# All weight operands of the first MLP's first unit made on ACT and POOL during the pooling, with sums in place

## The chip, the cores and the metric

The kernel runs on one core of a Trainium2 chip. Its five engines work from queues of their own, in order: PE (matrix products), DVE (vector), ACT (activations and copies), POOL (elementwise work on tiles in SBUF) and SP, which here issues every DMA. They wait for each other through semaphores. The metric is the device time of one execution in microseconds (us).

## The reference

Two residual layers on x of 1024 positions by 1024 channels, float32. Layer 0 mixes tokens by a centred pooling of four window sizes, layer 1 by differential attention. Each is followed by a gated MLP, and a root-mean-square norm stands ahead of each sub-layer:

```python
h = h + mixer(rms_norm(h, mix_norm[i]))
g, u = split(rms_norm(h, ffn_norm[i]) @ w_up[i], 2)      # 1024 -> 2 * 2816
gc = conv_b + sum(conv_w[j] * shifted(g, j))             # three taps along the sequence
h = h + (gelu(gc) * u) @ w_down[i]
```

After the second layer comes one more norm. Only layer 0, between its pooling and the first columns of its MLP, is touched by the change.

## The kernel before

**Precision.** A float32 operand of a product is split into two float32r tiles: hi is a copy made on ACT, lo is the operand less hi, made on DVE or POOL. A product is then three matmuls (hi·hi, lo·hi, hi·lo).

**The up projection.** The 2816 columns are worked in 22 units of 128 columns of g and 128 of u. A unit is a two by two block product, the channels in two halves and the sequence in two halves, done with seven products instead of eight (numbers 1 to 7; 12 matmuls of 128x512 each). The weight side needs seven operands: u1, u2, g2 as loaded, and four sums, s1 = g1+g2 (product 5), s2 = s1-u1 (product 6), u1-g1 (product 7), u2-s2 (product 3). Each is split into hi and lo. The x side needs seven as well: x1 and x2 come from the first four row tiles of 128 positions, x3 to x7 from sums of tiles 0 to 3 with tiles 4 to 7. PE runs the products of a unit in the order 1, 6, 2, 7, 5, 4, 3.

**Preparing a unit's weights.** `load` issues the two loads of a unit's weights (`raw`, 512 KB each) on SP. `prep` is a generator that makes the seven operands. For unit 0 its four sums are on DVE (L394) and five of its seven lo parts too (L380); for later units sums and lo parts are on POOL. The sums go into buffers `s`, the parts into buffers `wc`.

**Around it.** The pooling goes by halves of the sequence. `pool_band` makes the pooled values as band products (L828), one block `pl` of 128 channels after the other, each split into hi (ACT, L131) and lo (DVE, L132). `pool_proj` multiplies one row tile of 128 positions (L848, accumulators `pp`), `add_halves` adds to the residual (DVE, L175) and squares (ACT, L176), `rstd` makes the norm's factor in small DVE and ACT steps (L188 to L198, `ss`, `ms`, `rt`, `rs_p`, `rs_q`, `rs_r`), and `norm_to_x` scales the rows (ACT, L292, `xs`), turns them on PE (L299, `tp`) and makes the x operands: products with the gain (`b`, L309 on DVE, L331 on ACT), for tiles 4 to 7 the sums `t`, `b`, `xf` (DVE, L340 to L344), then hi (ACT, L304) and lo (L305, on POOL for x1 to x4 and x7, on DVE for x5 and x6; x1 of the first layer on POOL too).

**Order.** In this stretch no order is written by hand: a scheduler lays the instructions into each engine's queue by priority and by its own idea of durations, and the queue then runs as it is laid. `next(mlp)` runs the MLP's generator up to its next `yield`, so that its instructions are recorded at that place in the program, ahead of `pool_band(1)`. From unit 1 on the order of PE, DVE and ACT is the written one. Buffers that are used again later make their next user wait: `cm`, `wd` and `g` belong to the up stage (sums of the gated values, the down weights, the g values of a unit); the raw weights of unit 0 of this layer lie in two of the three `g` buffers.

The accumulators of the attention, the rest of the up stage and the down stage are as they were, and so is each engine's order there.

## Time and profile before

| what | value |
|---|---|
| median of 3 runs | 2084.54 us (2083.7 to 2086.34) |
| the profiled execution's own time | 2089.84 us |
| its span, first to last instruction | 2088.0 us |
| mean granted clock | 0.983 |
| PE busy | 2003.6 us (96%) |
| DVE busy | 1560.6 us (75%) |
| ACT busy | 1024.4 us (49%) |
| POOL busy | 895.3 us (43%) |

A row of the timeline gives the start and the length in us, the engine, the line of the kernel, the operation, the tile written and the tiles read, and the shape; behind it in brackets stands how long the engine was idle before, and what ended that. An `xN` row is N such instructions in a row. Instructions on one engine follow each other a little faster than their lengths say, since the tail of one overlaps the head of the next. A row of the table of windows gives a stretch, its length, and for each engine the busy time and the number of instructions, then PE's granted clock, the DMA share and the GB/s.

### The profile page before, as it was taken

The numbers are of one execution on the slowest core, as the hardware profiler recorded it, in microseconds if no ns is written. First come the engines' busy times: TensorE is split into PE (matmuls) and PEld (weight loads), VectorE is DVE, ScalarE is ACT, GpSimd is POOL, SyncE is SP. The second block draws the span as 40 slices with busy tenths as digits, with TensorE's granted clock in tenths as the row PEclk, the third lists the DMA queues.
The fourth block names the chain that finished last, engine by engine and source line by source line (L and its number), as shares of the span: only waits on it lengthen the run. The fifth ranks groups of instructions, "written<-read, shape, count | busy, mean of one in ns | idle before, by whom it ended". The sixth has DMA issues, their size and how long they took to land.

```text
span 2088.0 us, 27647 instructions
## 1 busy us (share of the span) xinstructions
PE 2003.6 (96%) x9659; PEld 1665.6 (80%) x9659; DVE 1560.6 (75%) x2294; ACT 1024.4 (49%) x1838; POOL 895.3 (43%) x676
## 2 busy tenths in 40 slices
PE   5789999999999999999999998997999999999998
PEld 5768888888888877888888887875888888888886
DVE  6877777777665748899899888778667777775665
ACT  5743333333443645676667666456433333334443
POOL 4489999997000000101110110114999999930000
PEclk7889999999999999999999999999999999999999
DMA  4226445454876512122212115253345545458663
GB/s 153 99 70 198 141 154 184 132 177 151 334 239 221 207 56 66 48 75 61 61 46 77 54 35 197 101 172 118 121 160 167 172 149 179 142 191 334 201 211 132
DMA packets 221720, 301.90 MB, mean 145 GB/s; under 512 B 17852, under 2 KB 142092, under 8 KB 218764
## 3 DMA queue, kind: packets, MB, share of 16 engines
q1 hardware_dynamic: 221580, 300.13, 44.0%
q8 instruction: 76, 1.25, 0.2%
q14 instruction: 64, 0.52, 0.1%
HBM read 196.78 MB, written 90.70 MB: 138 GB/s over the span
## 4 chain that ended last, share of the span: by engine, by line
PE 59%; DVE 5%; ACT 2%; DMA 2%; issue 1%; SPq 1%; POOL 0%; ACTq 0%; DVEq 0%; POOLq 0%
PE dn L596 14%; PE up_b L422 8%; PE pj L1027 7%; PE up_c L422 5%; PE up_a L422 5%; PE sc L1113 5%; PE pj L1069 4%; PE po L1155 3%; PE aT L1144 3%; PE pj L1251 2%; DVE nm L1115 1%; DMA kf<-t 1%; ACT prob L1118 1%; DMA raw<-in_ffn_w_up_dram 0%; PE wo_acc L1251 0%
## 5 line engine op out<-in xcount | busy, mean ns | idle before, releaser
L1095 POOL TENSOR_TENSOR q_lo<-qt,q_hi 128x256 fp32r<-128x256 f32 x64 | 49.6, 776 | 683.4 <-ACT q_hi L1094 351.0
L380 POOL TENSOR_TENSOR w_lo<-s,w_hi 128x512 fp32r<-128x512 f32 x168 | 273.9, 1630 | 17.7 <-ACT w_hi L379 17.2
L596 PE MATMUL dn<-hnT_hi 128*128 128x512 f32 x560 | 218.3, 390 | 0.4 <-DVE hda L617 0.2
L596 PE MATMUL dn<-hnT_lo,hnT_hi 128*128 128x512 f32 x560 | 217.9, 389 | 0.0
L596 PE MATMUL dn<-hnT_hi,hnT_lo 128*128 128x512 f32 x560 | 217.9, 389 | 0.0
L422 PE MATMUL up_b<-x_hi,w_hi 128*128 128x512 f32 x528 | 207.2, 392 | 5.8 <-ACT x_hi L304 4.6
L422 PE MATMUL up_b<-x_lo,w_hi 128*128 128x512 f32 x528 | 206.4, 391 | 2.3 <-DVE x_lo L305 2.3
L380 POOL TENSOR_TENSOR w_lo<-raw,w_hi 128x512 fp32r<-128x512 f32 x130 | 195.1, 1501 | 30.0 <-ACT w_hi L379 26.5
L422 PE MATMUL up_b<-x_hi,w_lo 128*128 128x512 f32 x528 | 206.2, 391 | 0.0
L379 ACT CAST w_hi<-s 128x512 fp32r<-128x512 f32 x176 | 108.4, 616 | 179.1 <-PE up_b L422 87.3
L1115 DVE TENSOR_REDUCE nm<-sc 128x1 f32<-128x1024 f32 x128 | 155.8, 1217 | 15.7 <-PE sc L1113 15.0
L579 ACT CAST hnT_hi<-mst 128x1024 fp32r<-128x1024 f32 (+1 forms) x76 | 74.7, 983 | 164.7 <-PE dn L596 123.1
L1118 ACT ACTIVATE prob<-sc,nm 128x1024 f32<-128x1024 f32 x128 | 142.7, 1115 | 23.3 <-DVE nm L1115 11.6
L580 DVE TENSOR_TENSOR hnT_lo<-mst,hnT_hi 128x1024 fp32r<-128x1024 f32 (+1 forms) x76 | 86.5, 1138 | 90.1 <-ACT hnT_hi L579 90.1
L422 PE MATMUL up_a<-hnT_hi,w_hi 128*128 128x512 f32 x352 | 139.3, 396 | 1.4 <-ACT g L499 0.9
L422 PE MATMUL up_a<-hnT_lo,w_hi 128*128 128x512 f32 x352 | 138.8, 394 | 0.1
L422 PE MATMUL up_a<-hnT_hi,w_lo 128*128 128x512 f32 x352 | 138.5, 394 | 0.0
L394 POOL TENSOR_TENSOR s<-raw 128x512 f32<-128x512 f32 x84 | 133.1, 1584 | 10.3 <-DMA raw<-in_ffn_w_up_dram 4.1
L422 PE MATMUL up_c<-hnT_hi,w_lo 128*128 128x512 f32 x352 | 137.1, 389 | 0.3 <-DVE w_lo L380 0.3
L422 PE MATMUL up_c<-hnT_hi,w_hi 128*128 128x512 f32 x352 | 136.9, 389 | 0.0
L422 PE MATMUL up_c<-hnT_lo,w_hi 128*128 128x512 f32 x352 | 136.9, 389 | 0.0
L596 PEld LDWEIGHTS dn<-hnT_hi 128*128 128x128 f32 x560 | 105.1, 188 | 22.9 <-DVE hda L617 1.2
(304 smaller groups left out, 5433.3 us busy)
## 6 DMA issues: line engine op xcount, KB each, us to landing
raw<-in_ffn_w_up_dram SPq DMA_DIRECT2D x88, 512.0 KB, 4.3
mst<-m_dram SPq DMA_DIRECT2D x70, 512.0 KB, 6.2
wd<-in_ffn_w_down_dram SPq DMA_DIRECT2D x22, 1024.0 KB, 6.0
wd_dram<-wd SPq DMA_DIRECT2D x22, 1024.0 KB, 6.4
m_dram<-cm SPq DMA_DIRECT2D x80, 256.0 KB, 5.6
wst<-wd_dram SPq DMA_DIRECT2D x40, 512.0 KB, 4.8
m_dram<-gc SPq DMA_DIRECT2D x66, 256.0 KB, 6.3
wst<-in_ffn_w_down_dram SPq DMA_DIRECT2D x30, 512.0 KB, 7.2
```

The costliest lines, as they stand in the source:

```text
L379: A.copy(hi, src)
L380: eng.tensor_tensor(lo, src, f32(hi), ALU.subtract)
L394: eng.tensor_tensor(t, a, b, op)
L422: PE.matmul(acc, l[a][:, k], r[b][:, k], start=first and n == 0, stop=n == 11, skip_group_check=True)
L579: A.copy(h_, x)
L580: V.tensor_tensor(l_, x, f32(h_), ALU.subtract)
L596: PE.matmul(banks[t], l[:, q, cols], r[:, q], start=first and cnt == 0, stop=stop and cnt == 3 * n - 1, skip_group_check=True)
L1027: PE.matmul(acc, l[:, k % 2, h], r[:, k], start=(n == 0), stop=(n == 3 * NK - 1))
L1069: PE.matmul(acc, l[:, k % 4], r[:, k], start=(n == 0), stop=(n == 3 * NK - 1))
L1113: PE.matmul(sc[:, ns_], l[:, c], ks[:, c, ns_], start=(l is qhi), stop=(l is qlo))
L1115: V.tensor_reduce(nm, sc, AX.X, ALU.max, negate=True)
L1118: A.activation(soft[j, i][c], sc, AF.Exp, bias=nm, accum_out=sm[:, c, i:i + 1])
```

## The change

For layer 0 the new `prep_first` makes all seven operands of unit 0 instead of `prep(0)`. Every sum and every lo part is on POOL and every hi part on ACT, as before. The four sums are written in place over the raw weights, so that no `s` buffer is used. Only operands 1 and 2 take `wc` buffers; 7 and 5 go into the buffer `cm`, 4 and 3 into `wd`, 6 into the third `g` buffer. The first step (1, 2 and 4) is recorded with the raised priority that it had for 1 and 2, and a second `next(mlp)` records all the rest right behind it, still ahead of `pool_band(1)`. Before, the rest was recorded after the pooling. Layer 1 goes on using `prep(0)`.

```diff
+READY = (0,)
@@ ffn
+        def pairs(where):
+            if where in ("cm", "wd"):
+                t = ar.tile(where, [P, 2, 2, 4, P], F32R, "w_hl")
+                return [(t[:, i, 0], t[:, i, 1]) for i in range(2)]
+            if where == "g":
+                t = ar.tile(where, [P, 2, 4, P], F32R, "w_hl")
+                return [(t[:, 0], t[:, 1])]
+            return [tuple(ar.tile(where, [P, 4, P], F32R, n) for n in ("w_hi", "w_lo"))]
+
-        def parts(src, eng=G):
-            hi, lo = (ar.tile("wc", [P, 4, P], F32R, n) for n in ("w_hi", "w_lo"))
+        def parts(src, eng=G, into=None):
+            hi, lo = into or pairs("wc")[0]
             A.copy(hi, src)
             eng.tensor_tensor(lo, src, f32(hi), ALU.subtract)
             return hi, lo
+
+        def prep_first():
+            w = ws.setdefault(0, {})
+            ru, rg = raws.pop(0)
+            u1, u2, g1, g2 = ru[:, 0:4], ru[:, 4:8], rg[:, 0:4], rg[:, 4:8]
+            room = {}
+            (room[7], room[5]), (room[4], room[3]) = pairs("cm"), pairs("wd")
...
+                room[1], room[2] = pairs("wc") + pairs("wc")
+                room[6], = pairs("g")
+            w[1] = parts(u1, G, room[1])
+            if not layer:
+                w[2] = parts(u2, G, room[2])
+            w[4] = parts(g2, G, room[4])
+            yield
+            for o, x, y, op, i in ((g2, g1, g2, ALU.add, 5), (g1, u1, g1, ALU.subtract, 7),
+                                   (u1, g2, u1, ALU.subtract, 6)):
+                G.tensor_tensor(o, x, y, op)
+                if i == 6:
+                    w[6] = parts(o, G, room[6])
+            for i, o in ((7, g1), (5, g2)):
+                w[i] = parts(o, G, room[i])
...
+            G.tensor_tensor(u2, u2, u1, ALU.subtract)
+            w[3] = parts(u2, G, room[3])
@@ ffn, at its start
-        first = prep(0)
+        first = prep_first() if layer in READY else prep(0)
         next(first)
-        if layer:
+        if layer and layer not in READY:
             next(first)
         yield
+        if layer in READY:
+            next(first, None)
+            yield
         load(1)
@@ trunk_kernel, between the two halves of the pooling
     with tc.high_priority(offset=100):
         next(mlp)
+    next(mlp)
     pool_band(1)
```

Where the instructions come to stand, at three places. The line numbers of the changed kernel are higher: L389 and L390 are the two lines of `parts`, L411 and L419 the sums, and the others are the old lines moved on (L131 to L132, L176 to L177, L305 to L306 and so on). `ha_174` to `ha_177` are the residual rows of tiles 4 to 7.

**First place: ACT and POOL at the end of the second `pool_band`.** `hnT_hi_69<-pl` are its eight blocks' hi parts on ACT, `w_hi` and `w_hl` weight parts. ACT before:

```order
L379 CAST w_hi<-raw 128x512
L131 CAST hnT_hi_69<-pl 128x512
L379 CAST w_hi<-raw 128x512
L131 CAST hnT_hi_69<-pl 128x512 x4
L176 ACTIVATE pp,ss<-ha_174 128x512 x2
```

ACT now:

```order
L389 CAST w_hi<-raw 128x512
L132 CAST hnT_hi_69<-pl 128x512
L389 CAST w_hi<-raw 128x512
L132 CAST hnT_hi_69<-pl 128x512
L389 CAST w_hl<-raw 128x512
L132 CAST hnT_hi_69<-pl 128x512
L389 CAST w_hl<-raw 128x512
L132 CAST hnT_hi_69<-pl 128x512
L389 CAST w_hl<-raw 128x512 x3
L132 CAST hnT_hi_69<-pl 128x512
L177 ACTIVATE pp,ss<-ha_174 128x512 x2
```

POOL before:

```order
L305 TENSOR_TENSOR hnT_lo_68<-xf,hnT_hi_67 128x4x128 x8
L380 TENSOR_TENSOR w_lo<-raw,w_hi 128x512 x2
L305 TENSOR_TENSOR hnT_lo_70<-b_990,hnT_hi_69 128x4x128
L305 TENSOR_TENSOR x_lo<-t_1059,x_hi 128x4x128
L305 TENSOR_TENSOR hnT_lo_70<-b_1053,hnT_hi_69 128x4x128
```

POOL now:

```order
L306 TENSOR_TENSOR hnT_lo_68<-xf,hnT_hi_67 128x4x128 x8
L390 TENSOR_TENSOR w_lo<-raw,w_hi 128x512 x2
L390 TENSOR_TENSOR w_hl<-raw,w_hl 128x512
L411 TENSOR_TENSOR raw<-raw 128x512 x3
L390 TENSOR_TENSOR w_hl<-raw,w_hl 128x512
L419 TENSOR_TENSOR raw<-raw 128x512
L390 TENSOR_TENSOR w_hl<-raw,w_hl 128x512 x3
L306 TENSOR_TENSOR hnT_lo_70<-b_1007,hnT_hi_69 128x4x128
```

Between the last blocks of the band ACT now has five more weight casts. Three of them ahead of the band's last block, and one ahead of the block before, read sums that POOL makes in the same stretch.

**Second place: tiles 6 and 7 on their way through the norm.** On DVE, the factor `rs_r` of tile 6 (its last step in these rows), with work of tile 5 around it. DVE before:

```order
L305 TENSOR_TENSOR hnT_lo_70<-b_989,hnT_hi_69 128x4x128
L196 SCALAR_TENSOR_TENSOR rs_q<-rs_p,rt 128x1
L344 TENSOR_TENSOR xf<-xf 128x512
L198 SCALAR_TENSOR_TENSOR rs_r<-rs_q,rt 128x1
L305 TENSOR_TENSOR x_lo<-xf,x_hi 128x4x128
L340 TENSOR_TENSOR t_1137<-b_1053,b_1052 128x512
L175 TENSOR_TENSOR ha_177<-pp,ha_177 128x512
```

DVE now:

```order
L345 TENSOR_TENSOR xf<-xf 128x512
L192 TENSOR_SCALAR ms<-ss 128x1
L193 RECIPROCAL rt<-rt 128x1
L306 TENSOR_TENSOR x_lo<-xf,x_hi 128x4x128
L195 TENSOR_TENSOR rs_p<-rt,ms 128x1
L341 TENSOR_TENSOR t_1154<-b_1070,b_1069 128x512
L197 SCALAR_TENSOR_TENSOR rs_q<-rs_p,rt 128x1
L176 TENSOR_TENSOR ha_177<-pp,ha_177 128x512
L199 SCALAR_TENSOR_TENSOR rs_r<-rs_q,rt 128x1
```

On ACT, the second square of tile 7 (`pp,ss<-ha_177`) behind the scaled rows `xs` of tile 6. ACT before:

```order
L292 ACTIVATE xs<-ha_176,rs_r 128x1024
L304 CAST x_hi<-t_1137 128x4x128
L176 ACTIVATE pp,ss<-ha_177 128x512
L331 ACTIVATE b_1130<-tp,gcol 128x128 x2
L190 ACTIVATE rt<-ss,eps 128x1
```

ACT now:

```order
L293 ACTIVATE xs<-ha_176,rs_r 128x1024
L305 CAST x_hi<-xf 128x4x128
L305 CAST hnT_hi_69<-b_1069 128x4x128
L332 ACTIVATE b_1147<-tp,gcol 128x128 x4
L305 CAST x_hi<-xf 128x4x128
L177 ACTIVATE pp,ss<-ha_177 128x512
```

The factor of tile 6 now stands behind an x_lo, a `t` and the residual add of tile 7. Tile 7's second square now stands behind tile 6's four `b`, which read tile 6's turned rows from PE.

**Third place: POOL at tile 7.** The lo parts of tile 7 are `hnT_lo_70` and `x_lo<-t` with the highest number and the last `x_lo<-xf`; `s` and `w_lo` belong to unit 1. POOL before:

```order
L305 TENSOR_TENSOR x_lo<-t_1215,x_hi 128x4x128
L305 TENSOR_TENSOR x_lo<-xf,x_hi 128x4x128 x2
L305 TENSOR_TENSOR hnT_lo_70<-b_1209,hnT_hi_69 128x4x128
L305 TENSOR_TENSOR x_lo<-t_1230,x_hi 128x4x128
L394 TENSOR_TENSOR s<-raw 128x512
L305 TENSOR_TENSOR x_lo<-xf,x_hi 128x4x128
```

POOL now:

```order
L306 TENSOR_TENSOR x_lo<-xf,x_hi 128x4x128
L433 TENSOR_TENSOR s<-raw 128x512
L433 TENSOR_TENSOR s<-s,raw 128x512
L433 TENSOR_TENSOR s<-raw 128x512
L433 TENSOR_TENSOR s<-raw,s 128x512
L390 TENSOR_TENSOR w_lo<-raw,w_hi 128x512
L390 TENSOR_TENSOR w_lo<-s,w_hi 128x512
L306 TENSOR_TENSOR hnT_lo_70<-b_1226,hnT_hi_69 128x4x128
L306 TENSOR_TENSOR x_lo<-t_1247,x_hi 128x4x128
```

Unit 1's four sums and two of its lo parts now stand ahead of tile 7's lo parts; before, one sum stood among them. On SP the load of the first down weights into `wd`, which was the sixteenth DMA of the program, now stands behind the raw loads of units 1 to 3.

More of the change, by code (lines that the diff above doesn't have):

```diff
@@ L381, in parts @@
             return hi, lo
+        def prep_first():
[4 more added lines that the diff above has]
+            (room[7], room[5]), (room[4], room[3]) = pairs("cm"), pairs("wd")
+            if layer:
+                room[1], room[6] = pairs("s") + pairs("s")
+            else:
+                room[1], room[2] = pairs("wc") + pairs("wc")
[12 more added lines that the diff above has]
+                w[i] = parts(o, G, room[i])
+            if layer:
+                yield
+                w[2] = parts(u2, G)
+            G.tensor_tensor(u2, u2, u1, ALU.subtract)
+            w[3] = parts(u2, G, room[3])
         def prep(j):
@@ L711, in ffn @@
         load(0)
-        first = prep(0)
+        first = prep_first() if layer in READY else prep(0)
         next(first)
-        if layer:
+        if layer and layer not in READY:
             next(first)
         yield
+        if layer in READY:
+            next(first, None)
+            yield
         load(1)
```

## The prediction

> **What bounds the kernel now.** I read the page's busy times and chain first, then the table of windows for the stretch that the change touches, then each engine's timeline there.
>
> ```profile
> PE 2003.6 (96%) x9659; PEld 1665.6 (80%) x9659; DVE 1560.6 (75%) x2294; ACT 1024.4 (49%) x1838; POOL 895.3 (43%) x676
> PE 59%; DVE 5%; ACT 2%; DMA 2%; issue 1%; SPq 1%; POOL 0%; ACTq 0%; DVEq 0%; POOLq 0%
> ```
>
> PE bounds nearly all of it. From unit 1 of the first MLP on, each engine's order is unchanged, so what the change is worth is how much earlier or later PE gets through unit 0. There PE is not the bound:
>
> ```profile
> 90.00:100.00 10.00, 1.97 (x8) 1.57 (x8) 10.00 (x19) 7.71 (x19) 5.25 (x4) 0.64 0.35 110
> 100.00:110.00 10.00, 6.78 (x21) 5.09 (x22) 9.97 (x11) 6.15 (x12) 8.12 (x5) 0.50 0.21 61
> 110.00:120.00 10.00, 5.15 (x13) 3.47 (x13) 10.00 (x12) 4.97 (x9) 6.76 (x5) 0.67 0.23 68
> 120.00:130.00 10.00, 9.11 (x39) 7.17 (x39) 4.41 (x5) 3.00 (x5) 9.86 (x8) 0.99 0.12 37
> ```
>
> PE (first busy number) idles 8.0, 3.2, 4.9 and 0.9 us while DVE (third) is busy throughout, until 120. That invites taking work off DVE. But whom does PE wait for?
>
> ```profile
> 94.01 1.97 PE L299 MATMUL tp<-ident,xs 128*128 128x128 f32 x8 [4.09 <-ACT xs L292]
> 102.05 1.97 PE L299 MATMUL tp<-ident,xs 128*128 128x128 f32 x8 [6.07 <-ACT xs L292]
> ...
> 114.57 0.80 PE L422 MATMUL up_b<-x_hi,w_hi 128*128 128x512 f32 x1 [4.02 <-ACT x_hi L304]
> ...
> 132.74 0.39 PE L422 MATMUL up_a<-hnT_hi,w_hi 128*128 128x512 f32 x1
> ```
>
> For the scaled rows of tiles 6 and 7 and then for x6, whose last piece comes from tile 7; unit 1 starts at 132.74. The x side is the late one, a chain from the pooled values through norm and sums of each tile. So I follow that chain.
>
> **Term A: the band's last block waits for POOL.** The nine POOL instructions that are added (four sums, five lo parts) look free: POOL idles 10.95 us there.
>
> ```profile
> 66.09 5.04 POOL L305 TENSOR_TENSOR hnT_lo<-xf,hnT_hi 128x512 fp32r<-128x512 f32 x4 [4.73 <-ACT hnT_hi L304]
> 71.09 2.53 POOL L380 TENSOR_TENSOR w_lo<-raw,w_hi 128x512 fp32r<-128x512 f32 x2
> 84.57 1.63 POOL L305 TENSOR_TENSOR hnT_lo<-b,hnT_hi 128x512 fp32r<-128x512 f32 x1 [10.95 <-ACT hnT_hi L304]
> ```
>
> One takes 5.04/4 = 1.26. Nine from 73.62 end at 84.96, and nothing on POOL is late. The casts on ACT are the trouble. They read POOL's sums, and ACT's queue has them ahead of the band's last cast.
>
> ```profile
> 72.26 0.59 ACT L131 CAST hnT_hi<-pl 128x512 fp32r<-128x512 f32 x1 [0.28 <-DVE pl L832]
> 73.68 0.58 ACT L131 CAST hnT_hi<-pl 128x512 fp32r<-128x512 f32 x1 [0.84 <-DVE pl L832]
> ```
>
> The raw weights are there in time, though by little:
>
> ```profile
> 59.69 6.22 SPq L374 DMA_DIRECT2D raw<-in_ffn_w_up_dram  x2
> ...
> raw<-in_ffn_w_up_dram SPq DMA_DIRECT2D x7, 512.0 KB, 3.9
> ```
>
> The second issue ends at 65.91, the load lands by about 69.8. POOL then does operand 4's lo, three sums, one lo and the fourth sum before ACT can cast operand 3: 73.62 + 6 x 1.26 = 81.18. With that cast (0.5, the 0.59 less the overlap) the band's last cast starts at 81.7 instead of 73.68. Behind it come its own 0.58, a DVE lo and three matmuls (0.69 and 0.5 or so, estimates from the next rows), so tile 4's second half, which DVE adds at 76.43 now, comes at 83.5: **+7.1**. Nothing hides this; all pooled rows of tiles 4 to 7 need that block. If POOL's six take 1.74 each, as beside DVE (row below), it is +10.0. Below 7.1 I see nothing, since 1.26 is POOL's pace when it is alone.
>
> ```profile
> 76.43 0.69 DVE L175 TENSOR_TENSOR ha<-pp,ha 128x512 f32<-128x512 f32 x1 [0.75 <-PE pp L848]
> ...
> 92.18 0.15 DVE L198 SCALAR_TENSOR_TENSOR rs_r<-rs_q,rt 128x1 f32<-128x1 f32 x1
> ...
> 93.45 0.68 DVE L175 TENSOR_TENSOR ha<-pp,ha 128x512 f32<-128x512 f32 x1
> ```
>
> **Term B: PE comes back slow.** It finishes what it has by about 78, then waits some 5 us for the block. After such a pause its matmuls run at half pace:
>
> ```profile
> 38.49 0.55 PE L828 MATMUL pl<-band,hnT_hi 128*128 128x256 f32 x1 [6.58 <-DVE hnT_lo L132]
> 38.84 0.42 PE L828 MATMUL pl<-band,hnT_lo 128*128 128x256 f32 x1
> 39.05 0.41 PE L828 MATMUL pl<-band,hnT_hi 128*128 128x256 f32 x1
> ...
> 45.16 0.28 PE L848 MATMUL pp<-pw_lo,hnT_hi 128*128 128x256 f32 x1
> 45.28 0.28 PE L848 MATMUL pp<-pw_hi,hnT_lo 128*128 128x256 f32 x1
> ```
>
> Steps of 0.21 instead of 0.12 us, for 6.5 us. Tile 4's scaled rows stand on ACT behind tile 5's squares, so tile 5's 24 matmuls count: 24 x 0.09 = **+2.2**; bounds 0 (no slow stretch) and 2.6 (all 6.5 us). The Trainium skill ("TensorE: Matmul & The Clock Gate", Part 1) has the gate open again after about 3.4 us of steady work; by that, an estimate, 16 matmuls would be slow and B would be 1.5, the whole sum 9.2. The row here shows almost twice as long, and I keep it.
>
> **Term C: the scheduler's new order.** On DVE, tile 6's factor moves from before an x_lo, a `t` and tile 7's add to behind them: from 92.18 to the end of the add, 94.05, that is **+1.9** (0 if those are done by then; 3.0 if one waits for POOL, +1.1 as below). On ACT, tile 7's second square stands 1.56 us behind tile 6's `xs` now:
>
> ```profile
> 92.81 1.15 ACT L292 ACTIVATE xs<-ha,rs_r 128x1024 f32<-128x1024 f32 x1
> ...
> 94.37 0.59 ACT L176 ACTIVATE pp<-ha 128x512 f32<-128x512 f32 x1
> ...
> 104.86 1.13 ACT L331 ACTIVATE b<-tp,gcol 128x128 f32<-128x128 f32 x4
> ```
>
> In the change it stands behind tile 6's turning on PE and four `b`: 1.15 + 1.97 + 1.13 + 0.6 for a cast = 4.85, **+3.3** for tile 7's factor, on which the last x6 hangs. Bounds 0 and 5.5 (two DVE instructions more, each +1.1).
>
> **Term D: what DVE loses.** The nine instructions that leave it:
>
> ```profile
> 81.94 0.69 DVE L394 TENSOR_TENSOR s<-raw 128x512 f32<-128x512 f32 x1 [0.24 <-ACT xs L292]
> ...
> 86.67 1.78 DVE L394 TENSOR_TENSOR s<-s,raw 128x512 f32<-128x512 f32 x1
> ...
> 95.14 1.75 DVE L394 TENSOR_TENSOR s<-raw 128x512 f32<-128x512 f32 x1
> ...
> 104.22 1.76 DVE L394 TENSOR_TENSOR s<-raw,s 128x512 f32<-128x512 f32 x1
> ...
> 111.52 0.68 DVE L380 TENSOR_TENSOR w_lo<-s,w_hi 128x512 fp32r<-128x512 f32 x1
> ...
> 116.67 2.37 DVE L380 TENSOR_TENSOR w_lo<-s,w_hi 128x512 fp32r<-128x512 f32 x2
> 118.96 1.76 DVE L380 TENSOR_TENSOR w_lo<-raw,w_hi 128x512 fp32r<-128x512 f32 x1
> 120.65 1.78 DVE L380 TENSOR_TENSOR w_lo<-s,w_hi 128x512 fp32r<-128x512 f32 x1
> ```
>
> Together 12.6 us. Only the first five, 6.7 us, stand before PE gets its last x6; the other 5.9 run beside product 6, and PE's idle time after 120 allows them **-0.9** (none, if it waits for something else). Of the 6.7, 1.78 against 0.69 for the same work says that DVE stood still for 1.1 us beside POOL:
>
> ```profile
> 86.16 1.74 POOL L305 TENSOR_TENSOR x_lo<-t,x_hi 128x512 fp32r<-128x512 f32 x1
> ```
>
> POOL's ended at 87.90, DVE's 0.55 later, at 88.45. So either the whole time is saved, or only some 0.6 each, 3.0, with the standstill left to DVE's next instruction. I take the middle, **-4.8**. The Trainium skill ("SBUF — State Buffer", SBUF: two separate sides) says that a DVE instruction with two SBUF inputs and a POOL one exclude each other for the whole instruction. By it the standstill belongs to POOL's and stays, D is -3.0 and the sum 11.7; the 0.55 above agrees with it.
>
> **Term E.** Unit 1's sums now run on POOL beside tile 7's four sums on DVE: 0 to 4 x 1.1 = 4.4. I take one, **+1.1**; that is a choice, since before, too, POOL ran beside them.
>
> **Hidden.** The down weights' load now waits until product 3 of unit 0 has read `wd`, which is when unit 1 starts.
>
> ```profile
> wd<-in_ffn_w_down_dram SPq DMA_DIRECT2D x22, 1024.0 KB, 6.0
> ...
> 140.74 1.18 DVE L442 TENSOR_TENSOR wd<-wd 128x512 f32<-128x512 f32 x1
> ```
>
> DVE first reads it 8.0 us into unit 1; issue (0.4) and landing take 6.4. Past the margin of 1.6 us DVE would stand with the eviction of product 7 behind it, and PE's product 4 waits for that one. `cm` and the third `g` buffer are needed later still. No DMA is added. ACT does as many casts as before.
>
> **Sum.** 7.1 + 2.2 + 1.9 + 3.3 - 4.8 - 0.9 + 1.1 = **+9.9**, with ends at 7.1 - 6.7 - 0.9 = -0.5 and 10.0 + 2.6 + 3.0 + 5.5 - 3.0 + 4.4 = +22.5. On the profiled execution's 2089.84 that is 2099.7; the runs' median is 5.3 below that execution, and 2084.5 + 9.9 = **2094.4**.
>
> **The rivals.** *DVE was the bound, and relief wins.* For it: DVE is busy without a gap from 90 to 120. Then all nine count, and the time is 2084.5 - 12.6 = 2072. It decides if the band's last cast starts before about 75, that is, if POOL's six end 6.5 us sooner than their pace allows. Against it: at 76.43 DVE waits for PE, so the feed sets the start. Chance 0.06.
>
> *The two cancel.* PE stays fast, the scheduler's order costs nothing, and the full 6.7 is saved: -0.5, 2084. Against it: the chain is laid in order, and in such a queue a stall is passed on. Chance 0.12.
>
> *Worse: unit 1's weights come late as well.* Their loads wait for `raw` buffers that tiles 4 and 5 free, so they move with the chain, and POOL's first sum of unit 1 now stands ahead of tile 7's lo parts. A load that lands after POOL gets there costs up to 0.4 + 3.9 there; with E in full (3.3 more) that is +17.5, 2102. Against it: POOL has three lo parts of tile 6 to do meanwhile. Chance 0.09.
>
> **How the numbers follow.** The forecast, slower by 4.5 to 15 (2089 to 2099.5), has 0.73. About 0.2%, 4.2 us, is what a measurement of this kernel can tell. Faster has 0.06, no change 0.12, slower 0.73 + 0.09 = 0.82. The range 2086 to 2102 leaves out the relief, most of the case that cancels, and the far end.
>
> **What would show it.** ACT's weight casts at the band's end waiting for POOL's sums, the last `hnT_hi<-pl` near 81.7; PE idle about 5 us before tile 4's last `pp`, then steps of 0.21; `xs` of tile 4 some 9 us later than now, that of tile 7 some 15; DVE with gaps where it had none; unit 1 starting near 142.6. I am wrong if the last `hnT_hi<-pl` is within 3 us of 73.68, or if unit 1 starts before 133.

## The result and the profile after

| kernel | median | runs | ratio to before |
|---|---|---|---|
| before | 2084.12 us | 2082.08 to 2086.34 | |
| changed | 2098.32 us | 2096.89 to 2100.7 | 1.0069 [1.0053, 1.0085] |

The change costs 14.2 us [11.0, 17.7]; 9.9 was forecast. The profiled execution took 2097.63 us, 7.8 more than before's, with a span of 2095.8. PE's busy time is the same as before to 0.5 us. From the page of the changed kernel, first part:

```profile
PE 2004.1 (96%) x9659; PEld 1666.3 (80%) x9659; DVE 1556.5 (74%) x2285; ACT 1024.0 (49%) x1838; POOL 901.9 (43%) x685
```

So PE waits longer, and it does so before unit 2 of the first MLP. To compare moments, traces are shifted so that the scaled rows of tile 3, ahead of all that the change touches, start together. Before's timeline and then the changed kernel's have:

```profile
64.35 1.15 ACT L292 ACTIVATE xs<-ha,rs_r 128x1024 f32<-128x1024 f32 x1 [0.89 <-DVE rs_r L198]
```

```profile
62.97 1.15 ACT L293 ACTIVATE xs<-ha,rs_r 128x1024 f32<-128x1024 f32 x1 [0.89 <-DVE rs_r L199]
```

The changed kernel's times move by +1.38; "aligned" means that. Unit 1 then starts near 146.5 (142.6 was forecast), and unit 2's first step on the gated values (ACT's `gc`) stands at 183.52 against 169.16: **+14.4**, all of the loss. (The two profiled executions are only 7.8 apart since 1.4 of it is the shift, and the stretch from layer 0's last unit to layer 1's first, the same instructions, took 931.3 us in the one trace and 936.6 in the other. Traces of the same work thus differ by 5 us far behind the change, and single runs by 4 or so; medians are used for totals, and aligned moments for places.)

**The band's end.** ACT's timeline of the changed kernel:

```profile
75.55 0.62 ACT L389 CAST w_hl<-raw 128x512 fp32r<-128x512 f32 x1 [3.49 <-POOL raw L411]
76.07 0.58 ACT L132 CAST hnT_hi<-pl 128x512 fp32r<-128x512 f32 x1
76.89 0.62 ACT L389 CAST w_hl<-raw 128x512 fp32r<-128x512 f32 x1 [0.24 <-POOL raw L411]
...
80.69 0.62 ACT L389 CAST w_hl<-raw 128x512 fp32r<-128x512 f32 x1 [1.82 <-POOL raw L419]
81.21 0.58 ACT L132 CAST hnT_hi<-pl 128x512 fp32r<-128x512 f32 x1
```

Each of these weight casts waits for a sum on POOL, and the band's last cast, which needs none of them, stands behind: 81.21, aligned 82.59, instead of 73.68. POOL's timeline shows the six instructions that it waits for, from 72.85 on, one behind the other, 7.8 us in all:

```profile
72.85 1.30 POOL L390 TENSOR_TENSOR w_hl<-raw,w_hl 128x512 fp32r<-128x512 f32 x1
74.23 3.99 POOL L411 TENSOR_TENSOR raw<-raw 128x512 f32<-128x512 f32 x3
78.17 1.27 POOL L390 TENSOR_TENSOR w_hl<-raw,w_hl 128x512 fp32r<-128x512 f32 x1
79.39 1.27 POOL L419 TENSOR_TENSOR raw<-raw 128x512 f32<-128x512 f32 x1
```

PE's timeline shows the pause and the slow stretch behind it, steps of 0.21 up to 86.49 and of 0.12 after:

```profile
81.84 0.58 PE L890 MATMUL pp<-pw_hi,hnT_hi 128*128 128x256 f32 x1 [4.03 <-ACT hnT_hi L132]
82.43 0.41 PE L890 MATMUL pp<-pw_hi,hnT_hi 128*128 128x256 f32 x1
82.65 0.41 PE L890 MATMUL pp<-pw_lo,hnT_hi 128*128 128x256 f32 x1
...
86.49 0.37 PE L890 MATMUL pp<-pw_hi,hnT_hi 128*128 128x256 f32 x1
86.69 0.28 PE L890 MATMUL pp<-pw_lo,hnT_hi 128*128 128x256 f32 x1
```

**Tiles 6 and 7.** DVE's timeline of the changed kernel; these are the factor's steps of tile 6 (first three) and tile 7, on 128x1 values:

```profile
99.00 1.24 DVE L195 TENSOR_TENSOR rs_p<-rt,ms 128x1 f32<-128x1 f32 x1
100.77 1.23 DVE L197 SCALAR_TENSOR_TENSOR rs_q<-rs_p,rt 128x1 f32<-128x1 f32 x1
...
102.52 0.72 DVE L199 SCALAR_TENSOR_TENSOR rs_r<-rs_q,rt 128x1 f32<-128x1 f32 x1
...
109.68 1.21 DVE L189 TENSOR_TENSOR ss<-ss 128x1 f32<-128x1 f32 x1
...
114.43 1.21 DVE L199 SCALAR_TENSOR_TENSOR rs_r<-rs_q,rt 128x1 f32<-128x1 f32 x1
```

Such a step takes 0.15 when POOL is still (92.18 in the prediction's rows). Before, one of each tile's was lengthened, by its timeline of DVE; now it is two or more:

```profile
90.44 1.21 DVE L196 SCALAR_TENSOR_TENSOR rs_q<-rs_p,rt 128x1 f32<-128x1 f32 x1
...
99.55 1.26 DVE L198 SCALAR_TENSOR_TENSOR rs_r<-rs_q,rt 128x1 f32<-128x1 f32 x1
```

**The last x operands.** DVE's timeline of the changed kernel in tile 7, and POOL's beside it:

```profile
119.71 1.49 DVE L341 TENSOR_TENSOR t<-b,b 128x512 f32<-128x512 f32 x1
121.28 1.59 DVE L342 TENSOR_TENSOR b<-b,xf 128x512 f32<-128x512 f32 x1
...
124.63 1.60 DVE L345 TENSOR_TENSOR xf<-xf 128x512 f32<-128x512 f32 x1
126.15 1.76 DVE L306 TENSOR_TENSOR hnT_lo<-b,hnT_hi 128x512 fp32r<-128x512 f32 x1
127.83 1.77 DVE L306 TENSOR_TENSOR x_lo<-xf,x_hi 128x512 fp32r<-128x512 f32 x1
```

```profile
120.61 1.71 POOL L390 TENSOR_TENSOR w_lo<-raw,w_hi 128x512 fp32r<-128x512 f32 x1
...
123.96 1.71 POOL L306 TENSOR_TENSOR hnT_lo<-b,hnT_hi 128x512 fp32r<-128x512 f32 x1
```

Two engines that each need 0.6 to 0.7 and 1.26 alone take turns: DVE's next large instruction starts every 1.5 to 1.7 us. PE waits for what comes out:

```profile
125.25 0.80 PE L461 MATMUL up_b<-x_hi,w_hl 128*128 128x512 f32 x1 [4.01 <-ACT x_hi L305]
...
129.66 0.79 PE L461 MATMUL up_b<-x_lo,w_hl 128*128 128x512 f32 x1 [0.47 <-DVE x_lo L306]
...
134.09 0.57 PE L461 MATMUL up_b<-x_hi,w_hl 128*128 128x512 f32 x1
...
145.14 0.39 PE L461 MATMUL up_a<-hnT_lo,w_hi 128*128 128x512 f32 x1
```

### The profile page after: what moved, and what is told of

Its sections match the earlier page's. It is cut to its first block, busy times and chain, and to the rows that moved or that the text cites. A ratio compares the mean times of both kernels' runs of the same rounds, so it can differ in the third digit from the quotient of the medians.

```text
span 2095.8 us, 27642 instructions
## 1 busy us (share of the span) xinstructions
PE 2004.1 (96%) x9659; PEld 1666.3 (80%) x9659; DVE 1556.5 (74%) x2285; ACT 1024.0 (49%) x1838; POOL 901.9 (43%) x685
## 4 chain that ended last, share of the span: by engine, by line
PE 84%; DVE 8%; ACT 3%; DMA 2%; issue 1%; SPq 1%; POOL 1%; ACTq 0%; DVEq 0%; POOLq 0%
PE dn L635 19%; PE up_b L461 17%; PE up_c L461 11%; PE up_a L461 11%; PE pj L1070 7%; PE sc L1156 5%; PE pj L1112 4%; PE po L1198 3%; PE aT L1187 3%; PE pj L1294 2%; PE pp L890 1%; DVE nm L1158 1%; DMA kf<-t 1%; PE tp L300 0%; DMA raw<-in_ffn_w_up_dram 0%
## 5 line engine op out<-in xcount | busy, mean ns | idle before, releaser
L390 POOL TENSOR_TENSOR w_lo<-s,w_hi 128x512 fp32r<-128x512 f32 x168 | 272.7, 1623 | 18.6 <-ACT w_hi L389 18.2
L390 POOL TENSOR_TENSOR w_lo<-raw,w_hi 128x512 fp32r<-128x512 f32 x130 | 192.9, 1484 | 41.7 <-ACT w_hi L389 38.5
L461 PE MATMUL up_b<-x_hi,w_hi 128*128 128x512 f32 x516 | 201.2, 390 | 1.5 <-DVE u L549 0.9
L461 PE MATMUL up_b<-x_lo,w_hi 128*128 128x512 f32 x516 | 200.9, 389 | 1.5 <-DVE x_lo L306 1.5
L461 PE MATMUL up_b<-x_hi,w_lo 128*128 128x512 f32 x516 | 200.7, 389 | 0.0
L389 ACT CAST w_hi<-s 128x512 fp32r<-128x512 f32 x172 | 105.9, 617 | 172.0 <-PE up_b L461 82.0
L1158 DVE TENSOR_REDUCE nm<-sc 128x1 f32<-128x1024 f32 x128 | 155.9, 1218 | 14.2 <-PE sc L1156 13.4
L1161 ACT ACTIVATE prob<-sc,nm 128x1024 f32<-128x1024 f32 x128 | 142.6, 1115 | 24.2 <-DVE nm L1158 11.8
L635 PEld LDWEIGHTS dn<-hnT_lo,hnT_hi 128*128 128x128 f32 x560 | 105.1, 188 | 21.9
```

Source lines behind the costliest of these rows:

```text
L389: A.copy(hi, src)
L390: eng.tensor_tensor(lo, src, f32(hi), ALU.subtract)
L461: PE.matmul(acc, l[a][:, k], r[b][:, k], start=first and n == 0, stop=n == 11, skip_group_check=True)
L635: PE.matmul(banks[t], l[:, q, cols], r[:, q], start=first and cnt == 0, stop=stop and cnt == 3 * n - 1, skip_group_check=True)
L1158: V.tensor_reduce(nm, sc, AX.X, ALU.max, negate=True)
L1161: A.activation(soft[j, i][c], sc, AF.Exp, bias=nm, accum_out=sm[:, c, i:i + 1])
```

## The experiments

Twelve kernels ran, each timed beside before on the same chip. The table has, aligned, the start of the band's last cast, of the scaled rows (`xs`) of tiles 4 to 7, of the first matmul on the last x6, of DVE's step on product 6 (`u`), and how much later than before unit 2 comes by the trace; then the timed difference to before with its 95% interval. All in us.

| kernel | last cast | xs 4 | 5 | 6 | 7 | x6 | u | unit 2 | timed |
|---|---|---|---|---|---|---|---|---|---|
| before | 73.7 | 80.8 | 84.4 | 92.8 | 100.8 | 114.6 | 122.3 | 0 | 0 |
| changed | 82.6 | 90.2 | 93.1 | 104.6 | 117.1 | 126.6 | 136.1 | +14.4 | +14.2 [11.0, 17.7] |
| 1 engine_only | 75.2 | 82.3 | 85.3 | 97.6 | 110.3 | 119.1 | 130.7 | +8.5 | +6.0 [3.3, 8.8] |
| 2 place_only | 81.0 | 88.2 | 89.2 | 91.2 | 110.3 | 119.7 | 129.2 | +7.7 | +7.1 [5.2, 9.2] |
| 3 casts_behind | 73.7 | 85.5 | 88.9 | 101.1 | 113.5 | 123.1 | 131.4 | +9.7 | +11.5 [7.5, 15.4] |
| 4 no_pool_u1 | 82.4 | 90.3 | 93.2 | 104.6 | 117.0 | 124.9 | 131.4 | +9.6 | +9.6 [6.0, 13.3] |
| 5 order_only | 81.9 | 88.9 | 91.8 | 99.5 | 106.4 | 120.6 | 127.8 | +7.9 | +8.1 [5.2, 11.3] |
| 6 casts_tile5 | 73.7 | 80.9 | 83.8 | 95.3 | 99.7 | 111.9 | 121.0 | +2.6 | +7.1 [4.4, 9.8] |
| 7 pool_extra | 75.2 | 83.4 | 87.0 | 96.5 | 105.2 | 119.8 | 127.6 | +5.2 | +3.5 [0.8, 6.3] |
| 8 order_before | 73.7 | 80.8 | 84.4 | 91.6 | 95.5 | 110.7 | 122.0 | +3.2 | +2.1 [-0.6, 4.6] |
| 9 x_lo_dve | 75.2 | 82.3 | 85.9 | 91.9 | 104.4 | 113.5 | 119.2 | -2.8 | -3.3 [-5.8, -0.8] |
| 10 after_x_lo_dve | 81.9 | 89.0 | 91.9 | 99.2 | 110.5 | 121.9 | 131.0 | +9.5 | +12.9 [9.8, 16.1] |
| 11 x_lo_dve_prio | 74.2 | 79.4 | 83.0 | 89.0 | 98.4 | 106.6 | 114.5 | -7.4 | -9.4 [-12.5, -6.5] |
| 12 one_cast_behind | 79.5 | 87.7 | 90.6 | 102.0 | 114.4 | 124.0 | 133.6 | +11.9 | +15.2 [12.3, 18.1] |

One thing differs between the traces that no edit made. After the same pause of 2.2 us, at 62.86 aligned, PE takes steps of 0.21 for some 3.4 us in the traces of the changed kernel and of kernels 1, 2, 4, 7 and 9, and steps of 0.12 in those of before and of 3, 5, 6, 8, 10 and 12 (11 has no such pause). Kernel 7 has before's order on every engine up to its first addition at 77.44, so the order is not the cause. The same matmul in PE's timeline of before and of kernel 7, aligned at the same moment:

```profile
64.14 0.28 PE L828 MATMUL pl<-band,xs_lo 128*128 128x256 f32 x1
```

```profile
62.88 0.41 PE L828 MATMUL pl<-band,xs_lo 128*128 128x256 f32 x1
```

Tile 3's operands come later by it. In kernels 1, 7 and 9 the band's last cast is 1.5 us late through it alone; the changed kernel has it at 82.6, kernels 5 and 10, with the same order up to there, at 81.9, and their `xs` 4 and 5 are 1.3 earlier. So single traces are compared within 1.5 us or so, and kernel 11, whose edit already moves `xs` 3 forward by 0.9, gains that much more than its row says.

### 1. The engine alone: unit 0's sums and lo parts on POOL, where they were recorded before

```diff
# against before
-                eng = (V, G)[j > 0]
+                eng = (V, G)[j > 0 or not layer]
```

> The kernel before, with one edit: the four sums and five lo parts of layer 0's unit 0 on POOL instead of DVE, where the program had them before (behind the pooling, sums in buffers of their own). No weight cast stands ahead of the band's last block, so the last hnT_hi<-pl should start within 1 us of before. DVE and ACT get tiles 4 to 7 in the order that the changed kernel has. By the prediction's own terms A and B are gone and C (+1.9, +3.3), D (-4.8, -0.9) and E (+1.1) stay: +0.6, 2084.7. By the sizes read in the changed kernel's trace (C 3.1 and 4.4, D -4.2, lo parts late 2.7, PE making up 1.3): +4.7, 2088.8. Rival, that it is the engine and not the place that costs: most of the 14.2 stays, 2095 or more. Rival, that the relief of DVE wins when the band isn't held: below 2080.

Measured: 1.0029 [1.0016, 1.0042], +6.0 us. The band's last cast is only the 1.5 us late just named, DVE has nine instructions less, and still it is slower. PE's timeline of this kernel near the x operands' end:

```profile
119.63 0.80 PE L422 MATMUL up_c<-hnT_hi,w_lo 128*128 128x512 f32 x1 [3.23 <-POOL w_lo L380]
```

PE now waits for weights from POOL. The scheduler also lays the late order of tiles 6 and 7 here (`xs` 6 and 7 come 12.3 and 12.7 behind the one ahead, 8.4 and 8.0 before): that order follows from DVE's relief, not from the place. So relief of DVE does not win even with the feed nearly on time.

### 2. The place alone: the same early place, sums and lo parts on DVE

```diff
# against the changed kernel, in prep_first
-                G.tensor_tensor(o, x, y, op)
+                V.tensor_tensor(o, x, y, op)
# likewise u2's sum, and parts(..., G, ...) of operands 4, 6, 7, 5 and 3
```

> The changed kernel, with the four sums in place and the five lo parts on DVE instead of POOL: same place in the program, same buffers, same casts. If the band's last cast is late because six POOL instructions of 1.26 us stand before the sums' casts (term A), DVE at 0.6 us each shortens that: the sums in place still wait for POOL's two lo parts of operands 1 and 2, which end near 72.9, so three or four DVE instructions and two casts later the last cast starts near 76, not 81.2: some 5 us less than the changed kernel, 2093, and less again (2089) if tiles 6 and 7 meet less of POOL. Rival, that the casts' place alone holds ACT whatever engine makes the sums: within 2 us of the changed kernel. Rival, that DVE needs the relief: slower than the changed kernel.

Measured: 1.0034 [1.0025, 1.0044], +7.1 us. The time is the one forecast, the way there is not: the band's last cast was to start near 76 and stays late, at 81.0, now behind DVE. DVE's and ACT's timelines of this kernel:

```profile
79.64 0.17 DVE L874 TENSOR_TENSOR pl<-pl,cons 128x8 f32<-128x8 f32 x1
```

```profile
79.84 0.59 ACT L132 CAST hnT_hi<-pl 128x512 fp32r<-128x512 f32 x1 [1.86 <-DVE pl L874]
```

The edge fix of the last block, 0.17 long, stands behind nine instructions of weights on DVE. Whichever of the two engines makes the weights, a queue with them ahead of the band delays it. In this kernel `xs` 6 follows 2.0 after `xs` 5: the delay was partly taken up there, and paid in tile 7.

### 3. The casts behind the band

```diff
# against the changed kernel: the second step moved, and its casts
# made to wait for the band's last block (a copy of one column)
-        next(mlp)
         pool_band(1)
+        next(mlp)
+            for i in (6, 7, 5, 3):
+                A.copy(room[i][0][:, 0, 0:1], f32(hnT[1][0][:, 7, 0:1]))
```

> The changed kernel with the rest recorded behind the band, and each of the four casts of a sum held back on ACT by a copy of one column of the band's last block into the cast's output (four small ACT instructions, overwritten by the casts). POOL does the same work from the same moment. The band's last cast should start at 72 to 73 as before, and PE should have no pause of 4 us ahead of tile 4. But the four casts now stand ahead of tile 4's first square, which waits for POOL's fourth sum: 73 plus five or six times 1.26, so near 80 instead of 75.7 before and 81.7 in the changed kernel. If what costs is ACT's queue being held for POOL's sums (my theory), tile 4's scaled rows come only some 2 to 4 us sooner and the time is 2094 to 2097. If what costs is the band's last block and PE's pause alone (rival), all of A and B comes back: 2089.

Measured: 1.0055 [1.0036, 1.0074], +11.5 us; 2.7 less than the change by the medians, within their intervals, and 4.7 less by the traces. The band's last cast is at 73.7 again, but tile 4 is late by 4.7 all the same. ACT's timeline of this kernel:

```profile
78.25 2.18 ACT L389 CAST w_hl<-raw 128x512 fp32r<-128x512 f32 x4 [4.26 <-POOL raw L413]
80.34 0.59 ACT L177 ACTIVATE pp<-ha 128x512 f32<-128x512 f32 x1
```

ACT stands for 4.26 us for POOL's third sum, and tile 4's square stands behind the four casts. The wait was not removed; it moved from in front of the band to in front of the norm.

### 4. Unit 1 without POOL

```diff
# against the changed kernel
-            eng.tensor_tensor(lo, src, f32(hi), ALU.subtract)
-            return hi, lo
+            eng is None or eng.tensor_tensor(lo, src, f32(hi), ALU.subtract)
+            return hi, (lo if eng else hi)
# prep: eng = None for j == 1 > layer, and no sum for it
```

> The changed kernel without unit 1's work on POOL in layer 0: its four sums are left out (its casts read the loaded weights) and its seven lo parts too (hi stands in for lo), so that unit of the output is wrong; everything else is as it was. It tells what tile 7 pays for POOL's work beside it (term E). In the changed kernel's trace tile 7's DVE instructions from t to x_lo take 1.49 to 1.77 us each. Theory, that this is waiting for POOL and lies on the path: they go back to about 0.7, x_lo is done some 3 to 5 us sooner, and the time is 2094 to 2095.5. Rival, that it is off the path, since PE has matmuls of products 2 and 3 to do meanwhile: within 1 us of the changed kernel. No theory expects a change ahead of tile 7's scaled rows.

This kernel leaves out unit 1's four sums and seven lo parts, so only its time is of use. Measured: 1.0046 [1.0029, 1.0064], +9.6 us. To `xs` 7 the trace is the changed kernel's to 0.2 us; of the 4.7 that come back 1.7 do so up to x6 and 3.0 up to `u`. DVE's timeline of this kernel:

```profile
125.37 0.68 DVE L306 TENSOR_TENSOR x_lo<-xf,x_hi 128x512 fp32r<-128x512 f32 x1
```

The last x_lo takes 0.68 instead of 1.77. The 4.7 are the price of unit 1's POOL work here; before had POOL work beside tile 7 too.

### 5. The order alone put back

```diff
# against the changed kernel
-        return add_halves(h[tt], accs)
+        with tc.high_priority(offset=60 * hf):
+            return add_halves(h[tt], accs)
```

> The changed kernel with one edit: the residual adds and squares of tiles 4 to 7 have a raised priority, so that tile 6's and tile 7's squares and factors stand where the kernel before had them or earlier (tile 7's second square ahead of tile 6's four b, tile 6's factor ahead of the x_lo). The weights are as in the changed kernel, and the band's last cast stays near 81. Queue theory (term C): in the changed trace the scaled rows of tile 6 come 11.5 behind tile 5's and tile 7's 12.4 behind tile 6's, against 8.4 and 8.0 before; with the order back both 3.1 and 4.4 come back, -7.5, 2090.8. Shared-time theory: DVE instructions with two operands in SBUF and POOL's shut each other out, so what counts is the sum of their times, and nine instructions moved from 0.6 on DVE to 1.26 on POOL add 5.9 whatever the order; then tile 7's rows come earlier, but its x operands no sooner than that sum allows, and the time is 2095 to 2098.

Measured: 1.0039 [1.0025, 1.0054], +8.1 us. Tiles 6 and 7 follow 7.7 and 6.9 behind instead of 11.5 and 12.4, which is 9.3 sooner. By the trace 6.5 of the 14.4 come back, 1.3 of them ahead of tile 5's rows, where the order is the same and PE was faster. From tile 5's rows to unit 2 it is 5.1, since the stretch from `xs` 7 to x6 grows from 9.6 to 14.2. So the order is a cost of its own, but only a good half of what it wins in the rows reaches the end: the time, 2094, lies between the two theories.

### 6. The second step's casts and lo parts behind tile 5

```diff
# against the changed kernel: next(mlp) for the second step behind
# pool_out of tile 7, its buffers first written after tile 5's x6
+            A.copy(room[i][0][:, 0, 0:1], ar.x[6][0][:, 0, 128:129])
```

> The changed kernel with the rest recorded behind the norms and the four casts of sums held back on ACT until tile 5's last x6 piece is cast (a copy of one column of it into each cast's output, overwritten by the casts). POOL makes the sums in place when it did. Now neither the band's last cast nor the squares of tiles 4 and 5 stand behind a cast that waits for POOL: A and B are undone altogether, so tiles 4 and 5 come as before, within 1 us. What is left of the 14.2 is the move to POOL and its new order. If these cost what the run with the engine alone moved showed (6.0), 2090 to 2092. Queue theory: with the sums out of DVE's way and no cast ahead of the norms, at most C (7.5) less D (4.2): 2086 to 2089. Rival, that moving early pays at last: 2082 or less.

Measured: 1.0034 [1.0021, 1.0047], +7.1 us. The band, tile 4 and tile 5 are as before, so terms A and B are gone, and the last x6 is even 2.7 early; then PE waits for its lo part. POOL's and PE's timelines of this kernel:

```profile
103.92 3.46 POOL L390 TENSOR_TENSOR w_hl<-raw,w_hl 128x512 fp32r<-128x512 f32 x2 [0.61 <-ACT w_hl L389]
```

```profile
116.35 0.80 PE L463 MATMUL up_b<-x_lo,w_hl 128*128 128x512 f32 x1 [3.58 <-DVE x_lo L306]
```

Lo parts at 1.73 on POOL beside tile 7 take what the earlier x6 had won. The trace has unit 2 only 2.6 late, the times say 7.1; this difference stays open.

### 7. Four more additions on an idle POOL

```diff
# against before
+        room = ar.tile("cm", [P, 4, 512], F32, "extra")
+        nc.gpsimd.tensor_tensor(room[:, tt - 4], h[tt][:, 0:512],
+                                h[tt][:, 512:1024], ALU.add)   # tiles 4 to 7
```

> The kernel before with four additional POOL instructions and nothing else: behind the recording of each of tiles 4 to 7 POOL adds the two halves of that tile's residual row (128x512, as large as a lo part) into a buffer that nothing reads until much later. Nobody waits for them but POOL's own queue. Shared-time theory: each takes 1.26 from DVE's two-operand instructions in a stretch where DVE has no gap, so four cost 3 to 5 us: 2087.5 to 2090. Queue theory: POOL idles 2.3, 1.4, 3.2 and 1.9 us between its instructions there, so most of the four is hidden: within 1.5 us of before.

Measured: 1.0017 [1.0004, 1.003], +3.5 us (+5.2 in the trace). No other engine waits for these sums, nothing is taken from DVE, and before had POOL idle there for part of the time. POOL's and DVE's timelines of this kernel:

```profile
97.08 1.71 POOL L881 TENSOR_TENSOR extra<-ha 128x512 f32<-128x512 f32 x1
```

```profile
97.59 1.75 DVE L394 TENSOR_TENSOR s<-raw 128x512 f32<-128x512 f32 x1
```

Of the trace's 5.2, 1.5 arose before the first addition, through PE's slow steps; the other 3.7, and the 3.5 by the times, are 0.9 an addition. A DVE instruction beside one is 1.1 longer. POOL's idle time was not free.

### 8. The order edit on the kernel before

> The kernel before with the same raised priority for the adds and squares of tiles 4 to 7. It tells whether the moment at which tile 7's scaled rows are ready sets the end, as the prediction's terms C and D take for granted. Tile 7's second square and factor stand earlier in ACT's and DVE's queue; its scaled rows should come 3 to 5 us sooner than 100.85. Queue theory: the last x6 and unit 1 come sooner by as much, 2080 to 2082. Shared-time theory: DVE was busy without a gap from 90 to 120 and has the same work, which only stands in another order; no gain, 2084 or some us more.

Same edit as in 5. Measured: 1.001 [0.9997, 1.0022], +2.1 us: no gain, perhaps a loss. `xs` 7 is 5.3 early and x6 3.9. PE's last matmul of product 6 is still 2.4 early (118.03 aligned against 120.41), but DVE's step on it (`u`) only 0.4. PE's timeline of before, then DVE's and PE's of this kernel:

```profile
120.41 0.40 PE L422 MATMUL up_b<-x_hi,w_lo 128*128 128x512 f32 x1
```

```profile
114.50 1.75 DVE L380 TENSOR_TENSOR w_lo<-s,w_hi 128x512 fp32r<-128x512 f32 x1
```

```profile
112.23 0.39 PE L422 MATMUL up_b<-x_hi,w_lo 128*128 128x512 f32 x1
...
116.91 0.73 PE L422 MATMUL up_b<-x_hi,w_hi 128*128 128x512 f32 x1 [2.93 <-DVE u L510]
```

Behind the x side the weights' lo parts on DVE are late next, lengthened by POOL, with `u` behind them. So before was not bound by the chain of tile 7's rows alone; that the work which DVE and POOL share is the bound fits this run, and 9 and 11 test it.

### 9 to 11. The opposite move: POOL's lo parts of the x operands on DVE

```diff
# against before (9) and the changed kernel (10)
-            put(7, t3, G)
+            put(7, t3, (V, G)[layer])
# likewise put(4, b21, G) and put(3, b22, G)
# 11, against before: also operands 1 and 2, and the order edit of 5 with offset=20 * hf
```

> The kernel before with the opposite move, and nothing of the change: the twelve lo parts of the x operands of tiles 4 to 7 that POOL made (x3, x4 and x7, three per tile) on DVE. POOL is then free from its last early weight part until unit 1's sums. DVE's own queue gets 12 instructions of about 0.6 more, 7.2, in the very stretch where it was busy without a gap. Theory of the relief (DVE is the bound there, and what leaves it helps): 2085 + 4 to 7, 2089 to 2092. Shared-time theory (DVE's two-operand instructions and POOL's shut each other out, so that each POOL instruction of 1.26 stands in DVE's way for its whole length): the sum falls by 12 x (1.26 - 0.6) = 7.9, and the time is 2077 to 2081. If the two only share part of the time: within 2 of before.

> The changed kernel with the same twelve lo parts on DVE. The band's last block stays late (about 82, A and B, some 8), since nothing there is touched. By the shared-time theory the rest of the 14.2 (6) comes back and some 2 more, as DVE has neither its sums nor POOL's lo parts against it: 2085 + 4 to 8, 2089 to 2093. By the relief theory DVE loses what the change gave it: 2098 or more.

> A version that is meant to beat both kernels: the kernel before with all lo parts of the first MLP's x operands on DVE, those of tiles 0 to 3 too, and a slightly raised priority of the adds and squares of tiles 4 to 7. The run with a raised priority alone gained nothing although tile 7's rows came 5 us sooner, since the lo parts then met more of POOL; with POOL out of the way they should not. By the shared-time theory it is 1 to 2 us better than the run with the twelve alone: 2075 to 2079. By the theory of the relief: 2090 or more.

Measured: 0.9984 [0.9972, 0.9996], -3.3 us; on the changed kernel 1.0062 [1.0047, 1.0077], +12.9; with all five operands and the order 0.9955 [0.994, 0.9969], **-9.4 us, faster than both kernels**. The table of windows of 11 in its 10 us up to tile 7's end; PE comes first, then its loads, DVE, ACT and POOL:

```profile
94.00:104.00 10.00, 2.75 (x10) 1.93 (x10) 10.00 (x22) 6.78 (x15) 0.00 (x0) 0.58 0.24 70
```

DVE does 22 instructions there, POOL none; before, in 90 to 100, it did 19 with POOL busy for 5.25. Kernel 11 is where it was forecast; kernel 9 wins less than half of the 7.9 that the theory gave. On the changed kernel the theory failed: 2089 to 2093 was forecast, and 2098 is what the rival named and cannot be told from the changed kernel by the times. Tile 4 is still 8.2 late and unit 1's POOL work still runs beside the last parts, but both were known; why no more came back stays open. Kernel 11 has three edits at once, so its 9.4 can't be shared out among them.

### 12. One cast less ahead of the band

```diff
# against the changed kernel: the second step behind pool_band(1);
# of ACT's rows only the cast of operand 3 changes its place
-        next(mlp)
         pool_band(1)
+        next(mlp)
```

> The changed kernel with the second step of the weights recorded behind the band instead of ahead of it. The order of PE and POOL is the same; on ACT one cast changes place: operand 3's, which waits for POOL's fourth sum, stands behind the band's last cast and no longer ahead of it. It is a dose of term A alone. In the changed kernel's trace that cast starts at 80.69 and the one ahead of it ends at 78.87, so the band's last cast should start near 79 instead of 81.21, 2.2 sooner. But tile 4's first square then stands behind operand 3's cast, at 81.2 instead of 81.7. If the band's last block sets the pace of tiles 4 and 5 through PE (terms A and B as predicted), all that follows comes 2 to 3 us sooner, 2095.5. If ACT's queue sets it (the square), 0.5 sooner, 2097.5 and not to be told from the changed kernel by the time; the traces tell the two apart by the scaled rows of tiles 4 and 5.

Measured: 1.0073 [1.0059, 1.0087], +15.2 us. In the trace the band's last cast is 3.1 earlier than in the change, and `xs` 4, 5, 6, 7, x6, `u` and unit 2 are 2.5 to 2.6 earlier, every one: what tile 4 wins passes down the chain undiminished. But the changed kernel's trace has PE's slow steps ahead of the band's end and this one has not; against kernels 5 and 10, which have not either, the last cast is 2.5 earlier and `xs` 4 and 5 only 1.2 or 1.3. How much a dose of term A is worth is thus not shown, and the times show no gain; 15.2 [12.3, 18.1] and 14.2 [11.0, 17.7] cannot be told apart, nor does the trace's 11.9 lie inside the first. Open. PE's timeline of this kernel:

```profile
80.00 0.58 PE L890 MATMUL pp<-pw_hi,hnT_hi 128*128 128x256 f32 x1 [1.58 <-ACT hnT_hi L132]
...
85.58 0.35 PE L890 MATMUL pp<-pw_hi,hnT_hi 128*128 128x256 f32 x1
```

## Why the prediction was right, and where it was short

The sign, the main mechanism and the range held: 2098.3 lies in 2086 to 2102 and in the forecast's own 2089 to 2099.5. The sum was short by 4.5 of 14.4, and some of the agreement is luck, as A and B show. The working, term by term, from the two aligned traces (one execution of each, so within 1.5 us or so):

| term | predicted | measured | from |
|---|---|---|---|
| A + B, band and slow PE | +9.3 | +8.7 | `xs` 5, 84.4 to 93.1 |
| C, tile 6 | +1.9 | +3.1 | `xs` 6 less `xs` 5 |
| C, tile 7 | +3.3 | +4.4 | `xs` 7 less `xs` 6 |
| D, DVE's nine | -4.8 | -4.1 | x6 less `xs` 7, 13.7 to 9.6 |
| E, unit 1's POOL | +1.1 | +3.0 | last matmul of product 6 less x6, 5.8 to 8.8 |
| the 5.9 beside product 6 | -0.9 | -1.3 | `u` less that matmul, 1.9 to 0.7 |
| behind `u` | 0 | +0.6 | unit 2 less `u`, 46.8 to 47.4 |
| sum | +9.9 | +14.4 | |

**A and B: right as a mechanism and in sum, not one by one.** The last cast was forecast at 81.7 and began at 82.59 aligned: POOL's six began 0.6 later than 73.62, behind PE's slow steps at tile 3, and took 7.8 instead of 7.6. Tile 4's second add (76.43 before) came at 84.69 aligned, 8.3 later and not 7.1. PE's pause was 4.03 (some 5 forecast), then 21 steps were slow by 0.09, 1.9 against 2.2, some of them ahead of that add; and 0.8 was won back by `xs` 5, since before's factor of tile 5 had a weight sum and a `b` ahead of it on DVE. Kernels 5 and 10, with the same order up to there, have +7.4 and +7.5 instead of +8.7. The Trainium skill ("TensorE: Matmul & The Clock Gate", Part 1) has PE at full pace after about 3.4 us of steady work; here the slow steps lasted 4.65 us, 6.5 before and 5.6 in kernel 12, so the traces have all three longer than that. Kernel 3 shows that ACT's wait is the cost and not the band's place alone: with the last cast back at 73.7, tile 4 is still 4.7 late. Kernel 6, which takes the wait away as well, has tiles 4 and 5 as before.

**C: the new order cost 7.5 instead of 5.2, and tile 6's share stood elsewhere.** For tile 6 the step "from 92.18 to the end of the add" priced three instructions more ahead of the factor on DVE. By the trace most of the 3.1 is on ACT: tile 6's second square, too, now stands behind tile 5's four `b` and two more casts, 4.21 behind `xs` 5 instead of 1.56. ACT's timelines of before (`xs` 5, that square) and of the changed kernel (`xs` 5, that square, `xs` 6, tile 7's second square):

```profile
84.40 1.15 ACT L292 ACTIVATE xs<-ha,rs_r 128x1024 f32<-128x1024 f32 x1
...
85.96 0.59 ACT L176 ACTIVATE pp<-ha 128x512 f32<-128x512 f32 x1
```

```profile
91.77 1.17 ACT L293 ACTIVATE xs<-ha,rs_r 128x1024 f32<-128x1024 f32 x1
...
95.98 0.59 ACT L177 ACTIVATE pp<-ha 128x512 f32<-128x512 f32 x1
...
103.27 1.15 ACT L293 ACTIVATE xs<-ha,rs_r 128x1024 f32<-128x1024 f32 x1 [1.29 <-DVE rs_r L199]
...
107.23 0.62 ACT L177 ACTIVATE pp<-ha 128x512 f32<-128x512 f32 x1
```

From the square to tile 6's scaled rows it is only 0.4 more than before (6.85 to 7.29). For tile 7 the square is 2.4 later behind `xs` 6 (3.3 forecast), and from it to `xs` 7 it takes 2.0 more (6.48 to 8.45): one more small step of 1.2 beside POOL (109.68) and an `xf` of 1.62 in its way. One of the standstills of 1.1 that the prediction kept for its upper end was thus due. Kernel 5 confirms the term, if not all of it: with the order back, 5.1 of the 7.5 reach unit 2. That the order comes with the relief of DVE and not with the place (kernel 1) was not foreseen.

**D: within its bounds,** between the -3.0 that the Trainium skill's rule gave ("SBUF — State Buffer", SBUF: two separate sides) and -6.7. The rule, that the two engines' instructions shut each other out, fits every DVE row of 1.5 to 1.8 us above. In part the standstill that left with the nine passed to others, C's and E's.

**E: too small by 1.9.** DVE's instructions of tile 7 take 1.49 to 1.77 us beside unit 1's sums and lo parts, so the last x_lo reaches PE 4.4 behind the first matmul on x6 instead of 1.6, and product 6 takes 3.0 longer. Kernel 4 gives 2.8 of these back when unit 1's POOL work goes, and 1.7 more ahead of x6, which the table has in D. The choice of "one" in a range of 0 to 4.4 was low.

**The -0.9: right, and a little more.** Before, DVE took product 6 up 1.9 after its last matmul, behind its own lo parts (120.65 in the prediction's rows); now it is 0.7.

**Hidden: right.** The down weights are first summed 8.6 us behind the first row of unit 1 above (153.74 on DVE), without a wait.

**The rivals.** *Relief wins* fell by more than the feed: its condition, the band's last cast before about 75, is met in kernels 3 and 6 (and missed by 0.2 in 1), and all three are slower. *The two cancel*: C cost 7.5, not nothing. *Worse, with unit 1's weights late*: its time of 2102 is near, its mechanism is not; POOL took unit 1's first sum without a wait.

**Behind the terms.** The prediction priced an instruction at 0.6 on DVE and 1.26 on POOL and asked which queue was late. In this stretch the two share one time: nine instructions moved from 0.6 to 1.26 add some 5.9 us to it (9 x 0.66). Kernel 1, where only the engine changes, costs 6.0; kernel 7 adds POOL work alone and costs; kernels 9 and 11 move work the other way and win. This fits all four in sign, and 1, 7 and 11 in size; 9 has less than half, and kernels 5 and 10 do not come where it put them (2095 to 2098 against 2094, 2089 to 2093 against 2098). So it is a direction and not yet a price. How much of kernel 1's 6.0 is the shared time and how much the orders that came with it was not measured apart.

## What to carry to other kernels

A cast that waits for a slow engine holds everything behind it on its own engine, so before work is moved into another engine's idle time, list what stands behind its consumers in their in-order queues. Where DVE and POOL work on the same stretch of two-input instructions, do not take the gaps of the one as free: on the kernel before it paid to put such work on the one that does it faster, even though that one looked full, and on the changed kernel no gain was clear of the noise. When a move changes what a scheduler believes, compare the laid order on every engine, since here the new order cost 7.5 by the trace, nearly as much as the wait.

## What the runs showed of the hardware that was not expected

- A DVE instruction on 128x1 values with two inputs takes 1.2 us instead of 0.15 when a POOL instruction on 128x512 is under way: small steps on a critical path pay the full standstill.
- Four POOL additions that nothing reads, put where POOL was idle, cost 3.5 us [0.8, 6.3].
- PE was slow for 5.6 us in kernel 12 after pauses of only 1.73 and 1.58 us, and for 4.65 us after one of 4.03: the pause need not be one long one.
- After one and the same pause of 2.2 us PE was slow in six traces and fast in seven, with the same order: a single trace can be 1.5 us late at one place through that alone.
